# Sub-keys of the last token group in another tile, dense tiles 736 bytes lower, and an order edge between key steps and a decoding

## The chip, the cores and the metric

The kernel runs on one core of one Trainium2 chip. The metric is the device time of one execution in microseconds (us), as the median of several runs.

## The reference, cut to what matters

One decoder layer for 1024 tokens of width 1024. A first half (modulated RMSNorm, one input projection, mLSTM heads and differential attention heads, output projection, gated residual) comes ahead. The second half is a product-key retrieval of experts, and the change lies there:

```python
def block(xb):                                  # 128 tokens
    q = (xb @ w_query).reshape(128, 8, 2, 128)
    s = jnp.einsum('thpk,hpnk->thpn', q, sub_keys)
    sv, si = lax.top_k(s, 16)
    cand = (sv[:, :, 0, :, None] + sv[:, :, 1, None, :]).reshape(128, 8, 256)
    cidx = (si[:, :, 0, :, None] * 128 + si[:, :, 1, None, :]).reshape(128, 8, 256)
    fv, fpos = lax.top_k(cand, 16)
    eidx = jnp.take_along_axis(cidx, fpos, axis=-1)
    g = jax.nn.softmax(fv, axis=-1)
    act = gelu(jnp.einsum('td,thkd->thk', xb, u_tab[eidx]))
    return jnp.einsum('thk,thkd->td', g * act, v_tab[eidx])
```

Each token so picks 16 of 16384 experts in each of 8 heads, and adds their rows of `v_tab` with weights. A residual and a final RMSNorm follow.

## The kernel before, in words

The 1024 tokens are 8 blocks of 128, in three groups: blocks 0 and 1, blocks 2 to 4, blocks 5 to 7. Each group goes through its front: projections and heads (`front_proj`, `front_mix`, `front_out`), `keys_load` (line 816, loads the sub-keys into two tiles `sk`), `front_norm2` (line 821: second norm, the transposed rows `h2T`, and for dense blocks a copy of them in HBM, `hT_d`) and `front_keys` (line 842). That last one makes four steps g of four half-heads each. A step projects the queries (`proj_T`, matmuls `ps_pj` of line 391, with the query weights `wr` loaded by SP in line 373, 32 loads in all for a group), evacuates them with ACT into `qp`, multiplies them with the sub-keys (`ps_s`, line 862), evacuates the scores (`s`, line 870), and takes the top 16 on DVE (`key_tops`, line 877, and `top16`). After a block's last step `found` (line 1442) decodes the picks (`route`, line 919).

The expert rows are then worked in two ways.

- Blocks 0, 1, 6 and 7 gather their rows. POOL issues indirect DMAs: `gu` (line 1006) for the rows of u, whose products DVE sums row by row (line 1010); `gv` (line 1058) for the rows of v of blocks 0 and 1, summed on PE (line 1072); `gvr` (line 1039) for those of blocks 6 and 7, summed on DVE (line 1046). Lines 1162 to 1180 close a gathered block (`gy`, `xo`: residual and final norm).
- Blocks 2 to 5 are dense. `gates` (line 1193) makes a 128 x 16384 matrix of gates for each out of one-hots: `gh` (line 1202), `oh` on DVE (lines 1237, 1238), `ps_g` on PE (line 1224), a copy on ACT (`stg`, line 1226) and a store to HBM (`G_d`, line 1229). Then `dense` (line 1253) sweeps over all 16384 experts in 128 steps j for the 512 tokens. It loads the transposed rows (`hTld`, line 1299) and splits them into a high part on ACT and a rest on DVE (`dhT`, lines 1300 and 1301). A step `s_mm` (line 1307) loads `u` (line 1310), splits it (`us`: ACT in line 1312; in line 1313 POOL in the first 18 steps, DVE after) and issues 24 matmuls `ps_dS` (line 1320) with a gelu behind them. A step `s_gate` (line 1323) multiplies with the gates `Gt`, loaded by `load_G` (line 1267), and a `v_step` (line 1340) loads and splits `dv`, and adds into `ps_dA` (line 1352). The sweep starts with 14 steps of `s_mm` (`AHEAD`), before the first `s_gate`; from the fourth of them on, three pieces of block 5's gates are traced behind each (`late`):

```python
        for j in range(AHEAD):
            with later(-HP if j < HJ else 0):
                s_mm(j)
            if j >= L0:
                for _ in range(LG):
                    with later(-LP), behind(LPACE):
                        next(late, None)
```

The order of instructions on each engine is not written out. The program is traced in the order of its text with a priority for each instruction (the sweep stands behind the front by `later(PD)`, and the late gates are put ahead by `later(-LP)`), and a scheduler picks, on each engine, the first by priority of those that its own model of times holds ready. So what an instruction must wait for decides where it stands. Besides data, a place in SBUF counts: tiles of the fronts and of the sweep are put at the same addresses, and the first write of a later tile must wait for the last reader of an earlier one that it overlaps. In the last group, blocks 5, 6 and 7 take each key step in this order. SP and POOL issue DMAs in the order of their lists.

In the program before, `dhT` takes bytes 110656 to 143424 of each partition, and the last group's two `sk` tiles lie at 114304 to 118400 and at 120448 to 124544. The tiles `g` end at 109920. The tile for transposed rows at 171872 to 184160 (tag `mT` or `hT`) is free in the last group's keys; `h2T` lies in the other one, at 184160 to 196448.

Of the kernel before, what the change touches and what calls it, by code (L numbers as in the profile page):

```python
# [8 lines left out]
F32 = mybir.dt.float32  # L9
# [12 lines left out]
P = 128  # L22
# [29 lines left out]
def kernel(ctx: ExitStack, tc: tile.TileContext, x, c_col, ada_w, ada_b, ada_bc, n1c,  # L52
# [223 lines left out]
    @contextmanager  # L276
    def behind(engines):

        traced = nc.cur_bb.bb.instructions
        n = len(traced)  # L280
        anchors = {}
        for i in reversed(traced[max(0, n - 600):]):
            if i.engine not in anchors and i.name not in own:
                anchors[i.engine] = i.name
                if len(anchors) == 5:
                    break
        yield
        info = mybir.DependencyInfo(mybir.DependencyClass.NoSync, mybir.DependencyReason.DATA)
        for i in traced[n:]:
            own.add(i.name)  # L290
            if i.engine in engines and i.engine in anchors:
                tc.add_manual_dep(i, anchors[i.engine], info, reason="pace")

    def tick():

# [354 lines left out]
    def group(t0, nb):  # L650
        o = Group()
        o.t0, o.nb, o.n = t0, nb, nb * P
        o.tr = [slice((t0 + b) * P, (t0 + b + 1) * P) for b in range(nb)]
        return o

# [158 lines left out]
            proj_R(w_out, half * 512, mT, nb, y_evac(half))  # L814

    def keys_load(o):
        o.sk = [fr.tile([P, 8, P], F32, tag="c8", name="sk", bufs=C8) for _ in range(2)]
        for i in range(2):
            nc.sync.dma_start(o.sk[i], skT[:, i * 8:i * 8 + 8, :])

# [21 lines left out]
    def front_keys(o, found):  # L842

        n, nb = o.n, o.nb
        o.rt = [route_start() for _ in range(nb)]
        for g in range(4):
            if g == N1G and o.k + 1 < len(gs):
                front_norm1(gs[o.k + 1])
            sk = o.sk[g // 2][:, g % 2 * 4:g % 2 * 4 + 4]
            q = {}  # L850

            def q_evac(f, ps):
                t = fr.tile([P, 512], F32, tag="t2", name="qp", bufs=T2)
                for i in range(f.stop - f.start):
                    q[f.start + i] = t[:, i * n:i * n + n]
                nc.scalar.activation(t[:, :(f.stop - f.start) * n].rearrange("p (f n) -> p f n", n=n), ps, AF.Copy)

            proj_T(wq, g * 512, o.h2T, nb, q_evac)
            for b in o.order:
                ps = bank("ps_s")  # L860
                for f in range(4):
                    nc.tensor.matmul(ps[:, f * P:(f + 1) * P], q[f][:, b * P:(b + 1) * P], sk[:, f],
                                     start=True, stop=True)
                if b == o.put_off:
                    if g == 0:
                        kept = fr.tile([P, 16, P], F32, tag="stg", name="s", bufs=SB)
                    s = kept[:, g * 4:g * 4 + 4]
                else:
                    s = fr.tile([P, 4, P], F32, tag="t2", name="s", bufs=T2)
                nc.scalar.activation(s, ps.rearrange("p (f n) -> p f n", f=4), AF.Copy)  # L870
                if b != o.put_off:
                    key_tops(o, b, g, s, found)
        if o.put_off is not None:
            for g in range(4):
                key_tops(o, o.put_off, g, kept[:, g * 4:g * 4 + 4], found)
# [377 lines left out]
    def dense(d1, d2, d3, d4, psS, psA):  # L1253
# [4 lines left out]
        NH = -(-n // 512)  # L1258
        hw = n // NH
        Gt = {}  # L1260
        d1.tile([P, 256], F32, name="pad")

        def load_G(j, parts=((0, na // TS),)):
            if parts[0][0] == 0:
# [169 lines left out]
    for k, o in enumerate(gs):  # L1434
        front_proj(o)
        front_mix(o)
        front_out(o)
        keys_load(o)
        front_norm2(o)
        last = k + 1 == len(gs)  # L1440

        def found(b, h0=0, nh=PH):
            tb, r = o.t0 + b, o.rt[b]
            dense_ = tb in DENSE
            route(r, dense_, tb in MIXED or (dense_ and last), h0, nh)
            if not dense_:
                if h0 == 0:
                    waiting.append(g_start(tb, r))
                    o.rt[b].blk = waiting[-1]
                indices(r.blk, h0, nh)  # L1450
                if not streams:
                    streams.append(gathers())
                    background.append([streams[0], RG, 0.0])
            elif h0 + nh == PH:
                gating.append((r.ii, r.g.rearrange("p h k -> p (h k)"), DENSE.index(tb), False))

        o.order = sorted(range(o.nb), key=lambda b: ((o.t0 + b in DENSE) != (last and ORDL), b))
        o.soon = o.order if SOG[k] else []
        o.part = SOG[k]
        o.put_off = o.order[-1] if k == 0 and DEF else None  # L1460
        front_keys(o, found)
        if not last:
            front_T(gs[k + 1])
        for b in o.order:
            if b not in o.soon:
                found(b)
        if k == 0:
            tables = all_gates()
            background.append([tables, RP, 0.0])
# [72 lines left out]
```

## Time and profile before

| | |
|---|---|
| median of 3 runs | 3030.85 us (3019.99 to 3034.86) |
| profiled execution | 3014.83 us, span 3012.7 us |
| PE busy | 2795.3 us (93% of the span) |
| DVE busy | 2382.6 us (79%) |
| POOL busy | 1280.1 us (42%) |
| ACT busy | 971.3 us (32%) |
| DMA | 900.00 MB, mean 299 GB/s |

Times within the profile are microseconds from the start of the span. The keys of the last group run up to about 1420, the dense sweep from there to the end. [...] A row of the timeline gives the start, the length and the engine of a run of like instructions. SPq is the queue of SyncE, which issues most DMAs; PEld are the weight loads of PE.

### The profile page before, as it was taken

How to read it: one execution, taken by the hardware profiler on the slowest of the kernel's cores; microseconds unless marked ns; L12 is line 12 of the kernel's file. 1: busy time of each engine (PE TensorE's matmuls, PEld its weight loads, DVE VectorE, ACT ScalarE, POOL GpSimd, SP SyncE). 2: the span in 40 equal slices, each digit the busy share in tenths (PEclk: the TensorE clock that was granted, in tenths of full speed). 3: DMA queues.
4: the chain of work that ended last, by engine and by line, in shares of the span. 5: the costliest groups of instructions: out<-in, count | busy, mean ns of one | idle time of the engine just before them, and what ended most of it. 6: DMA issues, size and time to landing. Idle time of an engine off the chain costs nothing.

```text
span 3012.7 us, 40060 instructions
## 1 busy us (share of the span) xinstructions
PE 2795.3 (93%) x13686; PEld 2087.7 (69%) x13686; DVE 2382.6 (79%) x5489; ACT 971.3 (32%) x1692; POOL 1280.1 (42%) x1083
## 2 busy tenths in 40 slices
PE   6899999599999989999797999999999999999998
PEld 5547757375566756665475877788777787777886
DVE  5634999847997677356998988899888899888956
ACT  1432244311244444222443322323222223222332
POOL 0000366654565443334556555455444454444300
PEclk9989999699999979999798999999999999999999
DMA  8745699899999887988799999999999999999942
GB/s 281 248 141 178 227 359 331 312 365 337 321 347 323 298 296 275 342 318 312 281 312 321 332 323 320 336 343 322 330 321 335 326 344 321 322 317 311 307 140 70
DMA packets 396848, 900.00 MB, mean 299 GB/s; under 512 B 34770, under 2 KB 184274, under 8 KB 392548
## 3 DMA queue, kind: packets, MB, share of 16 engines
q0 software_dynamic: 147456, 536.94, 49.6%
q1 hardware_dynamic: 249188, 360.51, 35.8%
q8 instruction: 108, 1.77, 0.2%
q14 instruction: 96, 0.79, 0.1%
HBM read 846.97 MB, written 50.35 MB: 298 GB/s over the span
## 4 chain that ended last, share of the span: by engine, by line
PE 44%; DVE 27%; DMA 15%; issue 9%; ACT 2%; POOL 2%; SPq 0%; DVEq 0%; POOLq 0%; ACTq 0%
PE ps_pj L391 10%; PE ps_pj L411 8%; PE ps_dA L1352 7%; DVE gu L1010 7%; DMA Gt<-G_d 6%; PE ps_dS L1320 6%; DVE ga L1046 4%; PE ps_g L1224 3%; PE ga L1072 3%; DMA gu<-in_peer_u_dram,ei 2%; DVE dvs L1346 2%; PE ps_S L593 2%; DVE dacc L1359 2%; DVE us L1313 2%; DVE W L1331 1%
## 5 line engine op out<-in xcount | busy, mean ns | idle before, releaser
L1006 POOL DMA_INDIRECT gu<-in_peer_u_dram,ei x512 | 651.7, 1273 | 958.7 <-DVE sv L894 346.6
L1352 PE MATMUL ps_dA<-dvs,W 128*128 128x512 f32 x2976 | 718.5, 396 | 46.2 <-DVE dvs L1346 18.5
L1320 PE MATMUL ps_dS<-dhT,us 128*128 128x512 f32 x3072 | 733.4, 393 | 11.1 <-POOL us L1313 8.9
L1010 DVE SCALAR_TENSOR_TENSOR gu<-gu,h2r 128x1024 f32<-128x1024 f32 x512 | 630.0, 1241 | 74.6 <-DMA gu<-in_peer_u_dram,ei 66.0
L1352 PEld LDWEIGHTS ps_dA<-dvs,W 128*128 128x128 f32 x2976 | 566.2, 191 | 176.5 <-DVE dvs L1346 22.3
L1320 PEld LDWEIGHTS ps_dS<-dhT,us 128*128 128x128 f32 x3072 | 581.7, 190 | 138.2 <-POOL us L1313 10.3
L1039 POOL DMA_INDIRECT gvr<-in_peer_v_dram,ei x256 | 302.4, 1181 | 314.2 <-DVE ga L1046 178.3
L1058 POOL DMA_INDIRECT gv<-in_peer_v_dram,eT x256 | 274.6, 1073 | 263.1 <-PE ga L1072 143.1
L1046 DVE SCALAR_TENSOR_TENSOR ga<-gvr,w,ga 128x1024 f32<-128x1024 f32 x254 | 325.3, 1281 | 1.5 <-DVE us L1313 0.4
L1345 ACT ACTIVATE dvs<-dv 128x512 fp32r<-128x512 f32 x248 | 155.2, 626 | 323.3 <-PE ps_dA L1352 169.7
L391 PE MATMUL ps_pj<-hT,wr 128*128 128x384 f32 (+1 forms) x768 | 234.7, 461 | 2.8 <-ACT ae L586 2.6
L391 PE MATMUL ps_pj<-h2T,wr 128*128 128x384 f32 (+1 forms) x768 | 231.2, 454 | 0.0
L1321 ACT ACTIVATE ge<-ps_dS 128x512 f32<-128x512 f32 x128 | 76.5, 598 | 441.7 <-PE ps_dS L1320 430.2
L1226 ACT ACTIVATE stg<-ps_g 128x512 f32<-128x512 f32 x128 | 133.9, 1065 | 242.4 <-PE ps_g L1224 162.9
L391 PEld LDWEIGHTS ps_pj<-hT,wr 128*128 128x128 f32 x768 | 145.4, 194 | 79.9 <-issue 9.0
L1329 DVE SCALAR_TENSOR_TENSOR ge<-ge,Gt 128x512 f32<-128x512 f32 x128 | 86.5, 685 | 137.2 <-DMA Gt<-G_d 115.2
L391 PEld LDWEIGHTS ps_pj<-h2T,wr 128*128 128x128 f32 x768 | 142.2, 190 | 74.4 <-issue 11.1
L411 PE MATMUL ps_pj<-wr,hT 128*128 128x256 f32 (+1 forms) x672 | 179.9, 421 | 4.6 <-DMA wr<-in_w_in_dram 3.7
L1346 DVE TENSOR_TENSOR dvs<-dv,dvs 128x512 fp32r<-128x512 f32 x248 | 168.1, 682 | 16.9 <-ACT dvs L1345 16.9
L1237 DVE TENSOR_TENSOR oh<-iotah,dT 128x1024 f16<-128x1024 f16 x128 | 92.0, 724 | 111.7 <-PE ps_g L1224 90.4
L1224 PE MATMUL ps_g<-oh 128*128 128x128 f16 x1024 | 138.6, 296 | 33.3 <-DVE oh L1238 14.5
L1072 PE MATMUL ga<-gv,strip 128*32 128x256 f32 x2048 | 150.7, 410 | 15.4 <-DMA gv<-in_peer_v_dram,eT 11.7
(292 smaller groups left out, 3304.0 us busy)
## 6 DMA issues: line engine op xcount, KB each, us to landing
u<-in_peer_uT_dram SPq DMA_DIRECT2D x128, 512.0 KB
dv<-in_peer_v_dram SPq DMA_DIRECT2D x248, 256.0 KB
wr<-in_w_in_dram SPq DMA_DIRECT2D x168, 256.0 KB
G_d<-stg SPq DMA_DIRECT2D x32, 1024.0 KB
Gt<-G_d SPq DMA_DIRECT2D x15, 2048.0 KB
wmod<-in_ada_w_dram SPq DMA_DIRECT2D x48, 512.0 KB
wr<-in_peer_w_query_dram SPq DMA_DIRECT2D x96, 256.0 KB
wr<-in_w_out_dram SPq DMA_DIRECT2D x48, 256.0 KB
```

The lines of the kernel that those rows point to most:

```text
L391: nc.tensor.matmul(out[f], w2[:, kh, f * P:(f + 1) * P], hT[:, kb, :n], start=kb == 0 and f % k == 0, stop=kb == NC - 1 and f % k == k - 1)
L411: nc.tensor.matmul(out[f], hT[:, kb, f * P:(f + 1) * P], wk[:, kh], start=kb == 0 and f % k == 0, stop=kb == NC - 1 and (f % k == k - 1 or ...
L1006: nc.gpsimd.indirect_dma_start(out=u, out_offset=None, in_=pu, in_offset=bass.IndirectOffsetOnAxis(ap=o.ei[:, k:k + 1], axis=0))
L1010: nc.vector.scalar_tensor_tensor(u, u, 1.0, o.h2, op0=OP.mult, op1=OP.mult, accum_out=o.z[:, k:k + 1])
L1039: nc.gpsimd.indirect_dma_start(out=vt, out_offset=None, in_=pv, in_offset=bass.IndirectOffsetOnAxis(ap=o.ei[:, k:k + 1], axis=0))
L1046: nc.vector.scalar_tensor_tensor(o.acc, vt, o.w[:, k:k + 1], o.acc, op0=OP.mult, op1=OP.add)
L1058: got = nc.gpsimd.indirect_dma_start(out=vt, out_offset=None, in_=pv, in_offset=bass.IndirectOffsetOnAxis(ap=o.eT[:, t:t + 1], axis=0))
L1072: mm = nc.tensor.matmul(o.acc[c * 32:(c + 1) * 32, q * QW:(q + 1) * QW], st[:, q, 31 + 32 * i - r:63 + 32 * i - r], vt[:, c * QW:(c + 1) * ...
L1224: nc.tensor.matmul(pg[:, r * P:(r + 1) * P], oh[:, 0, :, r], oh[:, 2 + i, :, r], start=i == 0, stop=i == np_ - 1)
L1320: nc.tensor.matmul(ps, us[:, a, c], hT[:, b, c, sl], start=c == 0 and i == 0, stop=c == NC - 1 and i == 2)
L1346: nc.vector.tensor_sub(vs[:, 1], v, vs[:, 0])
L1352: nc.tensor.matmul(pacc[tb], w[:, a, tb * P:(tb + 1) * P], vs[:, b], start=jj == 0 and i == 0, stop=jj == J - 1 and i == 2)
```

## The change

It has three parts. The last group's sub-keys go into one tile `skl` with the tag of the transposed rows, instead of two tiles with the tag `c8`; it lies at 171872 to 180064. The unused tile `pad` at the start of the sweep's first pool shrinks from 256 to 72 floats, so that all the sweep's tiles lie 736 bytes lower: `dhT` now takes 109920 to 142688, and begins where the tiles `g` end. And a new helper `after` puts an order edge, without a semaphore, on every DVE instruction of a `key_tops` that is traced after block 5's decoding: each of them may stand only behind the last DVE instruction of that decoding. Since block 5 is the first in each key step, these are the last key steps (g = 3) of blocks 6 and 7.

```diff
+    @contextmanager
+    def after(anchor):
+
+        traced = nc.cur_bb.bb.instructions
+        n = len(traced)
+        yield
+        if anchor is not None:
+            info = mybir.DependencyInfo(mybir.DependencyClass.NoSync, mybir.DependencyReason.DATA)
+            for i in traced[n:]:
+                if i.engine == ET.DVE:
+                    tc.add_manual_dep(i, anchor, info, reason="the dense block's routing goes first")
...
     def keys_load(o):
-        o.sk = [fr.tile([P, 8, P], F32, tag="c8", name="sk", bufs=C8) for _ in range(2)]
+        if o.k + 1 < len(gs):
+            o.sk = [fr.tile([P, 8, P], F32, tag="c8", name="sk", bufs=C8) for _ in range(2)]
+        else:
+            sk = fr.tile([P, 16, P], F32, tag="mT", name="skl", bufs=2)
+            o.sk = [sk[:, 0:8], sk[:, 8:16]]
         for i in range(2):
             nc.sync.dma_start(o.sk[i], skT[:, i * 8:i * 8 + 8, :])
...
                 if b != o.put_off:
-                    key_tops(o, b, g, s, found)
+                    with after(o.anchor):
+                        key_tops(o, b, g, s, found)
...
         Gt = {}
-        d1.tile([P, 256], F32, name="pad")
+        d1.tile([P, 72], F32, name="pad")
...
         def found(b, h0=0, nh=PH):
+            decode(b, h0, nh)
+            if last and o.t0 + b in DENSE and h0 + nh == PH:
+                o.anchor = next(i.name for i in reversed(nc.cur_bb.bb.instructions) if i.engine == ET.DVE)
+
+        def decode(b, h0, nh):
             tb, r = o.t0 + b, o.rt[b]
```

The lines of the changed program stand 12 to 18 lower; line 1299 is 1317, line 1010 is 1028, and so on. The scheduler's order moves with the change at three places.

On SP, at the end of the last group's query weights (`wr`), before: the sweep's loads `hTld` and `u` stand behind the last of them.

```order
L373 DMA wr<-in_peer_w_query_dram 128x2x256 x4
L1229 DMA G_d<-stg 128x2048 x2
L1299 DMA hTld<-hT_d 128x1024 x2
L1229 DMA G_d<-stg 128x2048
L1299 DMA hTld<-hT_d 128x1024 x2
L1310 DMA u<-in_peer_uT_dram 128x1024
```

The same list in the changed program, from 11 of the 32 query-weight loads on:

```order
L385 DMA wr<-in_peer_w_query_dram 128x2x256
L1317 DMA hTld<-hT_d 128x1024 x2
L385 DMA wr<-in_peer_w_query_dram 128x2x256 x2
L1247 DMA G_d<-stg 128x2048
L385 DMA wr<-in_peer_w_query_dram 128x2x256
L1317 DMA hTld<-hT_d 128x1024 x2
L385 DMA wr<-in_peer_w_query_dram 128x2x256 x5
L1328 DMA u<-in_peer_uT_dram 128x1024 x2
```

The `hTld` loads have moved ahead of 20 and 17 of the query-weight loads, and the first two `u` ahead of 12.

On POOL, where the first splits `us` of the sweep enter the gathers `gv` of block 1, before:

```order
L1058 DMA gv<-in_peer_v_dram,eT 128x1024 x118
L1313 TENSOR_TENSOR us<-u,us 128x1024 x2
L1058 DMA gv<-in_peer_v_dram,eT 128x1024 x4
L1313 TENSOR_TENSOR us<-u,us 128x1024
L1058 DMA gv<-in_peer_v_dram,eT 128x1024 x4
```

And in the changed program:

```order
L1076 DMA gv<-in_peer_v_dram,eT 128x1024 x54
L1331 TENSOR_TENSOR us<-u,us 128x1024
L1076 DMA gv<-in_peer_v_dram,eT 128x1024 x2
L1331 TENSOR_TENSOR us<-u,us 128x1024
L1076 DMA gv<-in_peer_v_dram,eT 128x1024 x36
L1331 TENSOR_TENSOR us<-u,us 128x1024
L1076 DMA gv<-in_peer_v_dram,eT 128x1024 x5
```

The first two splits have moved ahead of 64 and 62 gathers that they stood behind; the third stands behind 36 more.

On DVE, among the one-hots `oh` of block 5's gates, before (`gu,z` is a row sum of block 6):

```order
L1237 TENSOR_TENSOR oh<-iotah,dT 128x1024
L1238 TENSOR_TENSOR oh<-oh,dT 128x1024
L1010 SCALAR_TENSOR_TENSOR gu,z<-gu,h2r 128x1024
L1238 TENSOR_TENSOR oh<-oh,dT 128x1024
L1010 SCALAR_TENSOR_TENSOR gu,z<-gu,h2r 128x1024
L1237 TENSOR_TENSOR oh<-iotah,dT 128x1024 x2
L1238 TENSOR_TENSOR oh<-oh,dT 128x1024
```

And in the changed program, near the end of the one-hots:

```order
L1255 TENSOR_TENSOR oh<-iotah,dT 128x1024
L1256 TENSOR_TENSOR oh<-oh,dT 128x1024
L1028 SCALAR_TENSOR_TENSOR gu,z<-gu,h2r 128x1024 x2
L1255 TENSOR_TENSOR oh<-iotah,dT 128x1024 x3
L1256 TENSOR_TENSOR oh<-oh,dT 128x1024 x3
L1028 SCALAR_TENSOR_TENSOR gu,z<-gu,h2r 128x1024 x2
```

Between `gh` and the last one-hot stood 19 row sums of block 6; 4 stand there now, and the others follow behind. On PE, behind the last `ps_s` of the keys, one set of `ps_g` and sums of `gv` are now followed at once by 24 and 6 `ps_dS`, and then by 7 or 8 of them between sets of 8 `ps_g`; of the 384 `ps_dS` ahead of the first `ps_dA`, 39 stood behind the last `ps_g`, and none does now.

## Rows read from the trace of the kernel before

**Rows 1.** Windows: busy us (instructions) by engine, PE's clock, DMA share, GB/s.

```profile
core 0: us, PE busy (x) PEld busy (x) DVE busy (x) ACT busy (x) POOL busy (x), PEclk, DMA share, GB/s
1268.00:1413.80 145.80, 145.80 (x966) 87.87 (x965) 89.32 (x459) 36.76 (x51) 58.00 (x58) 1.00 0.88 308
...
1420.00:1494.30 74.30, 47.49 (x352) 29.18 (x350) 67.45 (x249) 29.08 (x29) 43.26 (x33) 0.72 0.86 314
1494.30:1607.50 113.20, 104.04 (x619) 83.36 (x620) 107.03 (x189) 58.73 (x65) 66.41 (x42) 0.94 0.87 289
1607.50:1638.80 31.30, 13.27 (x55) 10.15 (x54) 22.66 (x33) 5.70 (x8) 23.64 (x16) 0.74 0.97 352
1700.00:2000.00 300.00, 293.52 (x1271) 241.01 (x1270) 268.53 (x411) 89.18 (x135) 160.20 (x123) 0.98 0.94 331
...
2830.00:2930.00 100.00, 100.00 (x443) 82.81 (x442) 58.76 (x78) 33.40 (x49) 0.94 (x1) 1.00 0.57 186
```

**Rows 2.** Timeline, end of block 5's gates and first `ps_dA`: start, us, engine, line.

```profile
1606.38 0.68 DVE L1238 TENSOR_TENSOR oh<-oh,dT 128x1024 f16<-128x1024 f16 x1
...
1608.92 1.10 PE L1224 MATMUL ps_g<-oh 128*128 128x128 f16 x8
...
1611.26 0.33 SPq L1229 DMA_DIRECT2D G_d<-stg  x1
...
1638.78 1.65 PE L1352 MATMUL ps_dA<-dvs,W 128*128 128x512 f32 x3 [12.55 <-ACT W L1330]
```

**Rows 3.** Sources L1046 (last gathered rows) and L1313 (POOL splits): ns min/median/max, starts.

```profile
L1046 DVE SCALAR_TENSOR_TENSOR ga<-gvr,w,ga x254: 1268/1280/1291, 1897.3 to 2841.4; 128x1024 f32<-128x1024 f32 x127
...
L1313 POOL TENSOR_TENSOR us<-u,us x18: 2347/2640/3378, 1466.9 to 1630.6; 128x1024 fp32r<-128x1024 f32 x18
```

**Rows 4.** Timeline, first dense loads, last scores of the keys, first splits.

```profile
1416.21 1.39 SPq L1299 DMA_DIRECT2D hTld<-hT_d  x2
...
1418.98 2.94 PE L862 MATMUL ps_s<-sk,qp 128*128 128x128 f32 x24
...
1435.16 2.00 ACT L1300 ACTIVATE dhT<-hTld 128x1024 fp32r<-128x1024 f32 x2
...
1455.65 0.33 SPq L1310 DMA_DIRECT2D u<-in_peer_uT_dram  x1
...
1458.95 0.37 SPq L1310 DMA_DIRECT2D u<-in_peer_uT_dram  x1
...
1464.21 1.04 ACT L1312 ACTIVATE us<-u 128x1024 fp32r<-128x1024 f32 x1
...
1468.53 1.06 ACT L1312 ACTIVATE us<-u 128x1024 fp32r<-128x1024 f32 x1 [3.29 <-DMA u<-in_peer_uT_dram]
```

**Rows 5.** Groups of DVE in the sweep, 1700 to 2800: busy us, mean ns, idle.

```profile
L1046 DVE SCALAR_TENSOR_TENSOR ga<-gvr,w,ga 128x1024 f32<-128x1024 f32 x235 | 300.9, 1281 | 1.3 <-DVE us L1313 0.4
...
L1010 DVE SCALAR_TENSOR_TENSOR gu<-gu,h2r 128x1024 f32<-128x1024 f32 x201 | 241.8, 1215 | 4.9 <-DMA gu<-in_peer_u_dram,ei 4.9
```

**Rows 6.** Groups of DVE from 1420 to 1607.5.

```profile
L1010 DVE SCALAR_TENSOR_TENSOR gu<-gu,h2r 128x1024 f32<-128x1024 f32 x19 | 31.8, 1682 | 0.0
L1238 DVE TENSOR_TENSOR oh<-oh,dT 128x1024 f16<-128x1024 f16 x37 | 31.1, 867 | 0.0
L1237 DVE TENSOR_TENSOR oh<-iotah,dT 128x1024 f16<-128x1024 f16 x37 | 29.7, 813 | 6.4 <-PE ps_g L1224 6.4
...
L1301 DVE TENSOR_TENSOR dhT<-hTld,dhT 128x1024 fp32r<-128x1024 f32 x4 | 4.9, 1217 | 0.8 <-ACT dhT L1300 0.8
```

**Rows 7.** Sources L1172 and L1180, closing of gathered blocks, on DVE.

```profile
L1172 DVE SCALAR_TENSOR_TENSOR gy<-xo x8: 411/418/458, 1185.8 to 1546.7; 128x256 f32<-128x256 f32 x8
...
L1180 DVE SCALAR_TENSOR_TENSOR xo<-xo,gms,g2f x8: 477/480/485, 1192.5 to 1555.9; 128x256 f32<-128x256 f32 x8
```

**Rows 8.** Timeline of DVE, a row sum during a POOL split.

```profile
1598.48 3.42 DVE L1010 SCALAR_TENSOR_TENSOR gu<-gu,h2r 128x1024 f32<-128x1024 f32 x1
```

**Rows 9.** Groups of PE from 1422 to 1638.

```profile
L1320 PE MATMUL ps_dS<-dhT,us 128*128 128x512 f32 x384 | 99.8, 415 | 11.1 <-POOL us L1313 8.9 <-ACT us L1312 2.2
```

More of the change, by code (lines that the diff above doesn't have):

```diff
@@ L652, in group @@
         o.t0, o.nb, o.n = t0, nb, nb * P
+        o.anchor = None
         o.tr = [slice((t0 + b) * P, (t0 + b + 1) * P) for b in range(nb)]
```

## The prediction, made before the changed kernel ran

> **What bounds the kernel now.** I read the windows first. [Rows 1] cut the stretch in which the last group's keys end and the dense sweep of blocks 2 to 5 starts. In the keys stage (1268 to 1413.8 us) PE is busy all the time: 145.8 of 145.8 us. In the sweep itself (1700 to 2000) it is busy 293.5 of 300. Between them lies a hole: 47.5 of 74.3 us, 104.0 of 113.2 and 13.3 of 31.3. PE thus stands idle 26.8 + 9.2 + 18.0 = 54 us, while DVE is busy 67.5 of 74.3 and 107.0 of 113.2 us, 174.5 of 187.5 together. So the hole is bounded by DVE up to the last one-hot, which starts at 1606.4, and then by a chain: last `ps_g`, stage copy, store of G_d at 1611.3, load of it, gate product, first `ps_dA` at 1638.8 [rows 2]. Behind that the sweep runs on PE to its end, with gathers beside it until 2841 [rows 3] and without them after (226 ns a matmul there, 100 us over 443, against 236, 300 over 1271, [rows 1]). Whatever brings the first `ps_dA` forward therefore comes off the end, apart from what follows below.
>
> **Why the dense sweep's first steps lie in the hole.** The timeline of the queues [rows 4] shows that the first two loads of `hTld` are issued at 1416.2 and split at 1435.2, only after the last score matmuls of the keys (1419.0, 2.9 us). The address that `dhT` gets covers the last group's two sub-key tiles, so its first write must wait for the last matmul that reads them. The first `u` is issued at 1455.7 and split at 1464.2, and the first `ps_dS` comes behind that.
>
> **The change, part by part.**
>
> *Sub-keys in the other tile, dense tiles 736 bytes lower.* Both together let `dhT` begin where the gate tiles `g` end and no longer meet the sub-keys. By themselves they cost no instruction: two loads of the same size into another tile. The order is what changes. On SP the `hTld` loads move from behind all 32 query-weight loads to behind 12 and 15 of them, the first `u` behind 20. On POOL two of the 18 splits (`us`) move ahead of the keys' end. On PE 24 `ps_dS` and 6 more follow the last score matmuls almost directly; the 16 steps (384 `ps_dS`) still all stand before the first `ps_dA`, but none any more behind the last `ps_g`, where 39 stood. And on DVE the row sums `gu` of block 6, which now gets its gathers later because POOL still issues block 1's, shrink from 19 to 4 between `gh` and the last one-hot.
>
> What leaves the 187.5 us on DVE:
> - 15 row sums at their undisturbed 1.215 us [rows 5]: 18.2 us.
> - 4 splits of `dhT`, 4.9 us [rows 6], which go into the keys stage, where DVE is busy 89.3 of 145.8 us [rows 1]: covered there.
> - The last two gathered blocks' closing operations, now behind the last one-hot: 4 at 0.42 and 4 at 0.48 us [rows 7], 3.6 us. There DVE is idle 31.3 - 22.7 = 8.6 us, so they are covered; without the cover they would cost the 3.6.
> - What two POOL splits do to DVE, now ahead of 1420. The trace does not show that cost as a row; it is bounded by 0 and by 2 x 2.6 us (a split's whole length, [rows 3]). A row sum beside a split took 3.42 us at 1598.5 instead of 1.215 [rows 5, 8], so I take the difference, 2.2 each: 4.4 us.
> - Added: one more pair of one-hots, 0.81 + 0.87 = 1.7 us [rows 6].
>
> Sum: 18.2 + 4.9 + 3.6 + 4.4 - 1.7 = 29.4 us, and 174.5 would become 145. With the 13 us of idle time that DVE had, the stretch would be 158.
>
> [...]
>
> PE sets a second floor. It was busy 47.5 + 104.0 = 151.5 us in that stretch, and the 39 `ps_dS` from behind come in at about 0.24 us, 9 us: 161. So the stretch can shrink by 187.5 - 161 = 26 us at the prices of before. The granted clock was 0.72 in its first part [rows 1], and 384 `ps_dS` took 415 ns each by the record, 99.8 us [rows 9]; at the 236 ns of the sweep they would be 90.6. With PE kept busy, 9 us more could come. I don't count on it: PE still has to wait for one-hots and splits in turn.
>
> So the floors of the two engines allow 26 (PE) and 29 (DVE). Two engines that feed one another never both run without idle time; PE waited 11.1 us for splits alone [rows 9]. I take 2 to 3 us for that, and 24 remain.
>
> *What is given back later.* Block 6's row sums and all gathers behind them come later, by as much as the 15 that left: 15 gathers, some 38 us at the pace of the sweep (201 + 235 row operations in 1100 us, 2.5 us each, [rows 5]), and with the sweep starting 24 us earlier the gathers stand beside 62 us more of it. Beside gathers a matmul costs 4.4% more (236 against 226 ns): 2.7 us. The gathers end near 2880, still over 100 us before the end, so they don't become the bound.
>
> *The order edge (key step 3 of blocks 6 and 7 behind block 5's decoding).* Between block 5's own last key step and `gh` DVE has 190 instructions before and 189 after; four of the difference are the `dhT` splits and the rest one-hots. Block 6's keys and their decoding stand before `gh` as they did. So I price the edge at nothing. It could only cost if it held the other blocks' keys and made the gathers later, and those have 100 us to spare.
>
> *The tail behind the last `ps_g`* keeps its instructions: store, load, product. From 1608.9 to 1638.8, 30 us, unchanged [rows 2].
>
> **Sum.** 24 - 2.7 = 21 to 22 us. The profiled execution took 3014.8 us, 16 below the median of the three runs, 3030.9. Against its own time that gives about 2993, and against the median, in which the next runs will be told, 3009.
>
> **Rivals.**
>
> *A, slower: loads that block the keys stage.* SP and ACT work in order. The `hTld` loads now stand in the middle of the query-weight loads, and on ACT their splits and the first two of `us` stand between the evacuations of the keys' projections and scores. In [rows 4] an `hTld` came to its split 19.0 us after its issue, a `u` after 8.6 and 9.6. If ACT waits so in the new place, PE runs out of free banks, and in this stage PE has no idle time to give: twice 19.0 and twice 9 are 56 us in the worst case. Against it: the loads are issued long before their splits are due by the order, and the 19 us contain the wait for the sub-keys, which is gone. It decides from 24 us of PE idle time in 1268 to 1420 upwards; with 40 us of it the time would be 3047.
>
> *B, no change: the same work, waits in another place.* In the new order PE has 7 or 8 `ps_dS` between each set of one-hot matmuls. [...] DVE waited 6.4 us for `ps_g` already [rows 6]. If the 13 us idle become 35, the gain is 22 less, and 3028 to 3031 comes out. In its favour stand the 16 splits left, 2.6 us each; against it, that `dhT` and the first two splits are ready by 1420, so that PE starts ahead.
>
> *C, a larger gain.* If PE runs the stretch at full clock, the 9 us come on top, and if DVE loses its idle time too, the stretch is 145 us: a gain of 35 to 40, less 3: 2994 to 2999. The 54 us of idle PE time are the end of this side: 2980.
>
> *D, the order edge does not act or the lower tiles do not matter.* The order shows the moves, so only the price can fail; this falls under B.
>
> **How the numbers follow.** About 0.5%, 15 us, is what a measurement of this kernel can tell from no change; three runs lay 15 us apart. Forecast (gain of 15 to 28): 0.46. C: 0.18. B, with D and partial losses (gain under 15): 0.25. A: 0.11. Faster is the forecast with C, 0.64; same is B, 0.25; slower is A, 0.11. The range leaves out most of A and the end of C: 2984 to 3028.
>
> **What would show it.** Right: `hTld` issued before 1300; the first `ps_dS` within 5 us of the last score matmuls; PE idle in the keys stage under 3 us; PE's clock above 0.9 in the 75 us behind it; the last one-hot 22 to 28 us earlier, near 1580, and the first `ps_dA` near 1613; last row of the gathers near 2880. Wrong: PE idle in the keys stage by ACT's or SP's waits (A); last one-hot still near 1605 with DVE waiting for `ps_g` (B); or an early first `ps_dA` and yet the same end, which would say that the sweep's pace, not its start, sets the time.

## The result, and the profile after

The changed kernel takes 2989.23 us (median of 4 runs, 2983.2 to 2997.83) against 3026.49 us before (4 runs of the same series): ratio 0.9867, 95% interval [0.9844, 0.9891]. That is 37 us less, where the forecast gain was 21 to 22 us; the forecast's own ratio, 3009 to 3030.85, is 0.993, outside that interval. The time lies in the range that was given; the size of the gain was underestimated. The profiled execution took 2983.2 us with a span of 2981.3, 31.4 us below the span of before.

The windows of the changed kernel, in the stretches of [rows 1]: busy us (instructions) of each engine, PE's granted clock as a share of its full speed, DMA share, GB/s.

```profile
1268.00:1413.80 145.80, 145.80 (x955) 88.68 (x954) 97.36 (x480) 42.20 (x59) 59.49 (x54) 1.00 0.88 310
...
1420.00:1494.30 74.30, 68.66 (x452) 44.77 (x445) 72.97 (x240) 39.53 (x40) 48.09 (x35) 0.95 0.79 275
1494.30:1607.50 113.20, 86.68 (x604) 66.27 (x602) 84.35 (x122) 47.16 (x53) 57.52 (x41) 0.89 0.87 311
1607.50:1638.80 31.30, 26.02 (x98) 20.73 (x99) 28.00 (x48) 10.44 (x16) 10.89 (x9) 0.80 0.76 246
1700.00:2000.00 300.00, 297.53 (x1302) 245.00 (x1301) 269.03 (x414) 89.72 (x135) 164.88 (x124) 0.99 0.96 338
```

In the first 74 us behind the keys PE is now busy 68.7 us instead of 47.5, at a granted clock of 0.95 instead of 0.72. The row from 1607.5 is a trap: what stood at 1607 to 1638 before stands 28 us earlier now. Where a change moves work, stretches between the same instructions compare better. The same view of the kernel before, cut at the last scores of the first key step (1302.3), at those of the last (1421.9), at the last one-hot (1606.4) and at the first `ps_dA` (1638.8):

```profile
1302.30:1421.90 119.60, 119.35 (x833) 72.01 (x831) 81.08 (x450) 30.43 (x40) 51.87 (x52) 1.00 0.87 299
1421.90:1606.40 184.50, 148.52 (x949) 109.86 (x948) 172.28 (x430) 85.94 (x91) 107.21 (x74) 0.85 0.87 300
1606.40:1638.80 32.40, 14.37 (x60) 11.06 (x58) 23.76 (x35) 5.89 (x8) 24.50 (x17) 0.75 0.96 347
```

And of the changed kernel, cut at the same four instructions:

```profile
1302.40:1411.30 108.90, 108.90 (x722) 66.05 (x722) 82.70 (x448) 30.89 (x43) 47.73 (x44) 1.00 0.86 298
1411.30:1578.50 167.20, 161.25 (x1094) 114.98 (x1093) 146.60 (x384) 81.81 (x85) 92.79 (x67) 0.98 0.83 295
1578.50:1610.70 32.20, 2.48 (x19) 2.02 (x17) 20.50 (x37) 7.20 (x11) 16.86 (x13) 0.57 0.87 316
```

From the first scores to the first `ps_dA` it was 336.5 us and is 308.3: 28.2 less. PE's busy time went from 282.2 to 272.6 (9.6 less), its idle time from 54.3 to 35.7 (18.6 less), DVE's busy time from 277.1 to 249.8. Of the 35.7, 29.7 lie in the last row, behind the last one-hot. The work between these instructions is nearly the same, but not quite: of the one-hot products 24 fewer stand there (3.2 us at 0.132 us each), and of the sums of `gv` 16 more (1.2 us at 0.078). Before, then in the changed kernel:

```profile
L1224 PE MATMUL ps_g<-oh 128*128 128x128 f16 x464 | 61.2, 296 | 18.2 <-DVE oh L1238 8.9 <-ACT stg L1226 5.5 <-DVE cand L913 3.7
L1072 PE MATMUL ga<-gv,strip 128*32 128x256 f32 x720 | 55.9, 427 | 8.6 <-DMA gv<-in_peer_v_dram,eT 8.0 <-issue 0.6
...
L1242 PE MATMUL ps_g<-oh 128*128 128x128 f16 x440 | 58.5, 296 | 0.3 <-issue 0.3
L1090 PE MATMUL ga<-gv,strip 128*32 128x256 f32 x736 | 54.4, 394 | 0.3 <-DMA gv<-in_peer_v_dram,eT 0.3
```

The timeline of the changed kernel shows the mechanism, against [rows 4]: the loads of `hTld` are issued 131 us earlier, `dhT` is split while the keys still run, and the first `ps_dS` follow the last scores with 1.9 us between them, where it was 43 us.

```profile
1285.38 1.46 SPq L1317 DMA_DIRECT2D hTld<-hT_d  x2
...
1296.17 1.05 ACT L1318 ACTIVATE dhT<-hTld 128x1024 fp32r<-128x1024 f32 x1
...
1410.80 0.49 PE L879 MATMUL ps_s<-skl,qp 128*128 128x128 f32 x2
...
1413.15 3.01 PE L1338 MATMUL ps_dS<-dhT,us 128*128 128x512 f32 x12
```

Sources of the changed kernel, in the manner of [rows 3]: POOL splits, last gathered rows.

```profile
L1331 POOL TENSOR_TENSOR us<-u,us x18: 2355/2396/2932, 1332.3 to 1584.2; 128x1024 fp32r<-128x1024 f32 x18
...
L1064 DVE SCALAR_TENSOR_TENSOR ga<-gvr,w,ga x254: 1276/1287/1297, 1906.7 to 2857.2; 128x1024 f32<-128x1024 f32 x127
```

Groups of DVE in the changed kernel, from the last scores to the last one-hot (1411.3 to 1578.5), against [rows 6]:

```profile
L1255 DVE TENSOR_TENSOR oh<-iotah,dT 128x1024 f16<-128x1024 f16 x38 | 38.0, 1011 | 18.4 <-PE ps_g L1242 18.4
L1256 DVE TENSOR_TENSOR oh<-oh,dT 128x1024 f16<-128x1024 f16 x38 | 25.1, 685 | 0.2
...
L1028 DVE SCALAR_TENSOR_TENSOR gu<-gu,h2r 128x1024 f32<-128x1024 f32 x4 | 4.7, 1221 | 0.0
```

The row sums went from 19 to 4, as the order said. DVE now waits 18.4 us for `ps_g` instead of 6.4. And on PE, from the first scores to the first `ps_dA`, against [rows 9]:

```profile
L1338 PE MATMUL ps_dS<-dhT,us 128*128 128x512 f32 x384 | 97.6, 402 | 1.2 <-POOL us L1331 1.2
...
L1370 PE MATMUL ps_dA<-dvs,W 128*128 128x512 f32 x1 | 0.8, 792 | 27.4 <-ACT W L1348 27.4
```

The waits for splits (11.1 us before) are gone to 1.2, and one long wait is left, 27.4 us ahead of the first `ps_dA`. The timeline shows what it is, against [rows 2]: the last store of gates, the load of them 9.5 us behind it, and the gate product 17.6 us behind the load.

```profile
1582.18 0.33 SPq L1247 DMA_DIRECT2D G_d<-stg  x1
...
1591.69 0.76 SPq L1285 DMA_DIRECT2D Gt<-G_d  x1
...
1609.29 4.30 DVE L1347 SCALAR_TENSOR_TENSOR ge<-ge,Gt 128x512 f32<-128x512 f32 x7 [6.89 <-DMA Gt<-G_d]
...
1610.70 2.07 PE L1370 MATMUL ps_dA<-dvs,W 128*128 128x512 f32 x4 [27.35 <-ACT W L1348]
```

### The profile page after: what moved, and what is told of

Its sections match the earlier page's. It is cut to its first block, busy times and chain, and to the rows that moved or that the text cites. A ratio compares the mean times of both kernels' runs of the same rounds, so it can differ in the third digit from the quotient of the medians.

```text
span 2981.3 us, 40087 instructions
## 1 busy us (share of the span) xinstructions
PE 2783.4 (93%) x13686; PEld 2076.9 (70%) x13686; DVE 2382.0 (80%) x5489; ACT 973.6 (33%) x1695; POOL 1282.8 (43%) x1083
## 4 chain that ended last, share of the span: by engine, by line
PE 50%; DVE 18%; DMA 13%; issue 11%; POOL 5%; ACT 2%; SPq 0%; DVEq 0%; POOLq 0%; ACTq 0%
PE ps_pj L403 11%; PE ps_dS L1338 9%; PE ps_dA L1370 9%; DMA Gt<-G_d 8%; PE ps_pj L423 7%; DVE gu L1028 4%; PE ps_g L1242 3%; PE ga L1090 3%; POOL gvr L1057 3%; DVE ga L1064 2%; DMA gu<-in_peer_u_dram,ei 2%; PE ps_S L605 2%; DVE dvs L1364 1%; DMA gv<-in_peer_v_dram,eT 1%; PE ps_tr L379 1%
## 5 line engine op out<-in xcount | busy, mean ns | idle before, releaser
L1370 PE MATMUL ps_dA<-dvs,W 128*128 128x512 f32 x2976 | 720.8, 396 | 56.9 <-ACT W L1348 27.4
L1370 PEld LDWEIGHTS ps_dA<-dvs,W 128*128 128x128 f32 x2976 | 566.1, 191 | 188.9 <-ACT W L1348 27.4
L1028 DVE SCALAR_TENSOR_TENSOR gu<-gu,h2r 128x1024 f32<-128x1024 f32 x512 | 620.1, 1222 | 72.3 <-DMA gu<-in_peer_u_dram,ei 59.1
L1255 DVE TENSOR_TENSOR oh<-iotah,dT 128x1024 f16<-128x1024 f16 x128 | 102.2, 804 | 118.5 <-PE ps_g L1242 94.7
L1364 DVE TENSOR_TENSOR dvs<-dv,dvs 128x512 fp32r<-128x512 f32 x248 | 171.9, 698 | 16.4 <-ACT dvs L1363 16.4
L423 PEld LDWEIGHTS ps_pj<-wr,hT 128*128 128x128 f32 x672 | 128.5, 197 | 45.4 <-issue 23.8
L1377 DVE TENSOR_TENSOR dacc<-dacc,ps_dA 128x512 f32<-128x512 f32 x240 | 156.1, 683 | 4.6 <-PE ps_dA L1370 4.6
```

The lines of the kernel that those rows point to most:

```text
L423: nc.tensor.matmul(out[f], hT[:, kb, f * P:(f + 1) * P], wk[:, kh], start=kb == 0 and f % k == 0, stop=kb == NC - 1 and (f % k == k - 1 or ...
L1028: nc.vector.scalar_tensor_tensor(u, u, 1.0, o.h2, op0=OP.mult, op1=OP.mult, accum_out=o.z[:, k:k + 1])
L1364: nc.vector.tensor_sub(vs[:, 1], v, vs[:, 0])
L1370: nc.tensor.matmul(pacc[tb], w[:, a, tb * P:(tb + 1) * P], vs[:, b], start=jj == 0 and i == 0, stop=jj == J - 1 and i == 2)
L1377: nc.vector.tensor_add(o, o, pacc[tb])
```

## The experiments

Theory 1 was: the gain comes from the end of the overlap between `dhT` and the sub-keys; PE gets dense steps to do while DVE makes block 5's one-hots, and what is left of the hole is PE's order and the chain behind the last one-hot. The rivals stand with each run. All profiles are cut at the same instructions as above; the columns are us between them.

| run | to first scores | keys, first to last scores | to last one-hot | to first `ps_dA` | sweep to the end | span |
|---|---|---|---|---|---|---|
| before | 1302.3 | 119.6 | 184.5 | 32.4 | 1373.9 | 3012.7 |
| e1 pad alone | 1306.1 | 119.9 | 184.1 | 32.8 | 1376.9 | 3019.8 |
| e4 edge and pad | 1311.7 | 120.7 | 175.9 | 30.1 | 1376.7 | 3015.1 |
| changed | 1302.4 | 108.9 | 167.2 | 32.2 | 1370.6 | 2981.3 |
| e2 without the pad | 1302.8 | 108.9 | 165.6 | 30.6 | 1366.7 | 2974.6 |
| e3 without the edge | 1307.6 | 108.9 | 163.9 | 29.0 | 1374.7 | 2984.1 |
| e5 `ps_dS` held | 1300.9 | 109.9 | 149.0 | 33.0 | 1366.6 | 2959.4 |
| e6 load split | 1307.7 | 108.9 | 165.4 | 27.1 | 1377.4 | 2986.5 |
| e7 both | 1311.8 | 108.9 | 149.8 | 34.8 | 1366.0 | 2971.3 |
| e8 splits on DVE | 1311.7 | 112.7 | 166.5 | 27.9 | 1377.6 | 2996.4 |
| e9 held, no edge | 1304.3 | 110.3 | 147.5 | 26.9 | 1368.3 | 2957.3 |
| e10 held less, split, no edge | 1315.0 | 108.9 | 150.9 | 29.4 | 1379.3 | 2983.5 |
| e11 fewer gathers | 1306.8 | 108.9 | 165.4 | 31.9 | 1355.1 | 2968.1 |

The first column varies by 14 us between programs whose order there is the same up to that point or nearly so, and the sweep by 11 us within nearly one order (e2 and e6): that is the scatter of single executions. The part from the first scores to the first `ps_dA` scatters less: 336.5 and 336.8 us in the two profiles of the old order (before, e1), 308.3 and 305.1 in two of the new (changed, e2). So it became 28 to 32 us shorter.

### e1: the pad alone

```diff
-        d1.tile([P, 256], F32, name="pad")
+        d1.tile([P, 72], F32, name="pad")
```

> The kernel before with only the sweep's tiles 736 bytes lower; the sub-keys stay in their two old tiles, and no order edge. Theory 1 (the end of the address overlap between dhT and the sub-keys makes the gain): dhT still meets the old sub-key tiles, so the order is that of before and nothing moves: last one-hot near 1606, first ps_dA near 1639, time within 0.5% of before (3011 to 3042). Rival (addresses themselves, or the row tile a2r that dhT no longer meets, matter): first hTld before 1416 and 10 us or more gained. Beside that it is a second profile of the order of before: how far its sweep, from first ps_dA to the end, lies from 1373.9 us, tells how much of the 3.3 us by which the changed kernel's sweep was shorter is scatter.

Measured: 3026.97 us, ratio 1.0014 [0.9996, 1.0031] against 3023.05 us (19 runs). No part of the kernel moves by more than the scatter. The lower tiles alone do nothing.

### e2: sub-keys and edge, the pad as before

```diff
-        d1.tile([P, 72], F32, name="pad")
+        d1.tile([P, 256], F32, name="pad")
```

> The changed kernel with the pad back at 256 floats: sub-keys in the other tile and the order edge. The order on every engine is that of the changed kernel. Theory 1: dhT now ends 448 bytes inside the row tile a2r, which is last read before the keys begin, so it costs nothing: last one-hot near 1578, first ps_dA near 1611, ratio to before near 0.987. Rival: the 736 bytes carry part of the gain, then 5 us or more are lost against the changed kernel and hTld or dhT show a wait in 1280 to 1320. Second profile of the changed order: its sweep from first ps_dA to the end against 1370.6.

Measured: 2980.14 us, ratio 0.9868 [0.9845, 0.9891], the same as the changed kernel's. So the 736 bytes carry nothing: the overlap that mattered is that with the sub-keys, and the one with the row tile does not.

### e3: the change without the order edge

```diff
-                    with after(o.anchor):
+                    with after(None):
```

> The changed kernel without the order edge. Theory 1: the edge is worth nothing, since between gh and the last one-hot DVE has 127 instructions with 4 row sums here, 126 with 4 in the changed kernel: last one-hot 1576 to 1581, ratio to before 0.984 to 0.990. Rival (the edge brings block 5's gates forward): gh 5 us or more later than 1483, last one-hot as much later.

Measured: 2985.59 us, ratio 0.9887 [0.9859, 0.9915]. The intervals lie over one another, so with the sub-keys moved the edge is not to be told from nothing. In the table the part from the last scores to the last one-hot is even 2 to 3 us shorter without it; the one-hots' last was expected between 1576 and 1581 and came at 1580.4. Since e1 shows the pad to be worth nothing, this run is close to the move of the sub-keys alone. It also bears on what paces the one-hots: DVE is busy 139.6 us there, 7.0 less than in the changed kernel (146.6), and the part is only 3.3 us shorter.

### e4: edge and pad, sub-keys in their old tiles

```diff
-        if o.k + 1 < len(gs):
+        if True:
             o.sk = [fr.tile([P, 8, P], F32, tag="c8", name="sk", bufs=C8) for _ in range(2)]
```

> The kernel before with the order edge and the lower tiles, sub-keys in their two old tiles: dhT still waits for the last score matmuls. Theory 1: no gain from it, hTld issued after 1400, 17 row sums ahead of the last one-hot, first ps_dA 1628 to 1640, time within 0.5% of before. Rival (DVE is relieved by the edge): last one-hot 10 us or more earlier than 1606.

Measured: 3011.97 us (10 runs), ratio 0.9956 [0.9939, 0.9974]: 11 us faster, which neither theory had. Its windows, from the first scores on:

```profile
1311.70:1432.40 120.70, 119.58 (x833) 71.99 (x831) 81.01 (x451) 30.15 (x40) 51.94 (x52) 1.00 0.85 296
1432.40:1608.30 175.90, 142.98 (x919) 103.90 (x919) 164.60 (x423) 81.20 (x86) 97.18 (x70) 0.85 0.89 305
1608.30:1638.40 30.10, 22.18 (x90) 17.12 (x88) 23.75 (x31) 9.62 (x14) 23.00 (x15) 0.87 0.92 319
```

`dhT` is as late as before (the keys take 120.7 us, PE's clock behind them is 0.85), yet the one-hots end 8.6 us sooner behind the last scores (175.9 against 184.5), and PE is busy 22.2 us instead of 14.4 in the last part, since 72 `ps_dS` stand behind the last `ps_g` there and 39 did before. Since e1 shows the pad to be worth nothing, this is the edge: it shifts the whole order of the late gates. So my price of nothing holds only beside the moved sub-keys. DVE's busy time in that part falls by 7.7 us, and its row sums alone from 31.8 us (19 at 1682 ns) to 22.8 (17 at 1347). Why they are cheaper in the new order was not followed further.

### e5: dense steps from 11 on held behind the last gates

```diff
         for j in range(AHEAD):
-            with later(-HP if j < HJ else 0):
+            if j == 11:
+                with later(-LP):
+                    for _ in late:
+                        pass
+                hold = next(i.name for i in reversed(nc.cur_bb.bb.instructions) if i.engine == ET.PE)
+            with later(-HP if j < HJ else 0), held(hold):
                 s_mm(j)
```

`held` puts an order edge like that of `after` on the PE instructions traced within it; steps 14 and 15 get it too.

> The changed kernel, with the ps_dS of the steps from 11 on ordered behind block 5's last ps_g on PE; 264 ps_dS stand ahead of it and 120 behind. Theory 1 (what is left of the hole is PE's: DVE waited 18.4 us for ps_g, and PE then stands idle 27.4 us ahead of the first ps_dA): last one-hot 10 to 18 us after 160 instead of 167 us from the keys' end, that is near 1563 where the keys end at 1411, PE busy in the 32 us behind it, first ps_dA near 1595, ratio to before 0.979 to 0.984. Rival (DVE sets the one-hots' pace, the waits are only gaps of it): last one-hot stays 167 us behind the keys' end, 120 ps_dS fill the tail for nothing, ratio 0.986 to 0.990.

Measured: 2965.22 us, ratio 0.9807 [0.9779, 0.9834]. From the last scores to the last one-hot it is 149.0 instead of 167.2 us, and the first `ps_dA` comes 16.4 us earlier behind the first scores (291.9 against 308.3). The windows, cut at the last scores (1410.8), the last one-hot and the first `ps_dA`:

```profile
1410.80:1559.80 149.00, 133.77 (x977) 93.44 (x975) 140.95 (x380) 75.89 (x77) 86.62 (x64) 0.94 0.87 311
1559.80:1592.80 33.00, 31.57 (x137) 25.07 (x136) 28.07 (x44) 15.89 (x21) 23.06 (x16) 0.92 0.96 336
```

DVE, busy 146.6 of 167.2 us in the changed kernel, is busy 141.0 of 149.0 here, and waits 6.3 us for `ps_g`:

```profile
DVE oh L1267 <- PE ps_g L1254: 6.3, 5, 2.9
```

Of the 18.2 us, 12.6 are idle time of DVE (20.6 against 8.0) and 5.6 its busy time: 11 POOL splits stand in that part instead of 14, and the first half of a one-hot takes 820 instead of 1011 ns. So in the changed kernel the one-hots were paced for the most part by PE, which did dense steps between them; the same steps fit in the 33 us in which PE waits for the gates' store and load. Theory 1 holds, and the bound passes back to DVE.

### e6: the last load of gates in three parts

```diff
-            load_G(0, ((early, na // TS),))
+            load_G(0, ((early, early + 4), (early + 4, na // TS - 1), (na // TS - 1, na // TS)))
```

> The changed kernel, with the last load of block 5's gates (eight token parts, 17.6 us from its issue to the first product) cut into three loads of 4, 3 and 1 parts, so that only the last eighth waits for the last store. Theory 1 (the tail behind the last one-hot is a chain of store, landing, load): the tail of 32.2 us becomes 20 to 25 us and as much comes off the end, ratio 0.983 to 0.985. Rival (the load's time is queueing behind gathers, not its size): tail 29 to 33 us, ratio as the changed kernel, 0.987.

Measured: 2985.9 us, ratio 0.9864 [0.9835, 0.9894]: no gain to be seen. The tail went from 32.2 to 27.1 us in the profile, 5 us instead of the 7 to 12 expected; and since it is 29.0 to 32.2 us in the four profiles without the split (changed, e2, e3, e11), as little as 2 of them may be the split's. The timeline of DVE ahead of the first product:

```profile
1602.29 1.23 DVE L1028 SCALAR_TENSOR_TENSOR gu<-gu,h2r 128x1024 f32<-128x1024 f32 x1 [3.33 <-DMA gu<-in_peer_u_dram,ei]
...
1606.53 1.23 DVE L1028 SCALAR_TENSOR_TENSOR gu<-gu,h2r 128x1024 f32<-128x1024 f32 x1
...
1607.68 4.92 DVE L1347 SCALAR_TENSOR_TENSOR ge<-ge,Gt 128x512 f32<-128x512 f32 x8
```

The product no longer waits for the load: it follows a row sum without a gap. Four row sums stand ahead of it on DVE, and wait for gathers themselves. Part of what the load gave went into this queue.

### e7: both

The edits of e5 and e6 together.

> Both of the last two in one kernel. If each works by itself and they add up: last one-hot near 1563, tail 20 to 25 us, first ps_dA near 1585, ratio 0.975 to 0.980. If the 120 ps_dS behind the last ps_g (28 us at 0.235) are longer than the shorter tail, PE sets it and the gain of the split load is lost: ratio as e5.

Measured: 2970.98 us, ratio 0.9811 [0.9786, 0.9835], as e5. The tail is 34.8 us, with PE busy 32.6 of it: the 120 `ps_dS` are longer than the chain that they cover, so the split load has nothing to give.

### e8: the first 18 splits on DVE

`UP`, the number of splits that POOL takes, goes from 18 to 0. DVE takes them: at the 1223 ns that its 110 other splits `us` take in the mean in the changed kernel, 18 are 22 us.

```diff
-    WB, T2, C8, KV, T4, RB, SB, OB, WLO, PB, LAG, DB, GD, AHEAD, LG, RH, ORDL, UP, LP, L0, DU, HP, HJ = 7, 8, 4, 2, 3, 3, 1, 2, 0, 5, 4, 2, 1, 14, 3, 4, 1, 18, 310000, 3, 28, 0, 0
+    WB, T2, C8, KV, T4, RB, SB, OB, WLO, PB, LAG, DB, GD, AHEAD, LG, RH, ORDL, UP, LP, L0, DU, HP, HJ = 7, 8, 4, 2, 3, 3, 1, 2, 0, 5, 4, 2, 1, 14, 3, 4, 1, 0, 310000, 3, 28, 0, 0
```

> [...] If a POOL split holds DVE for 2.2 us (my term of the sum), 16 of them in the stretch cost 35 us now, and taking them away and paying 22 leaves the last one-hot where it is or up to 13 us earlier. If they cost DVE little, the last one-hot comes up to 22 us later, less the 20 us in which DVE idled: later by 5 to 22 us, ratio 0.989 to 0.994. [...]

Measured: 2998.34 us, ratio 0.9904 [0.9872, 0.9936]. The part to the last one-hot is 166.5 us, as in the changed kernel (167.2), though DVE does 16 splits and 4 row sums more there. The window of that part and its groups on DVE:

```profile
1424.40:1590.90 166.50, 158.58 (x1094) 113.68 (x1092) 142.28 (x421) 86.00 (x89) 66.35 (x59) 0.98 0.89 314
...
L1255 DVE TENSOR_TENSOR oh<-iotah,dT 128x1024 f16<-128x1024 f16 x38 | 25.8, 690 | 17.4 <-PE ps_g L1242 15.9 <-issue 1.4
L1256 DVE TENSOR_TENSOR oh<-oh,dT 128x1024 f16<-128x1024 f16 x38 | 25.2, 688 | 0.0
L1331 DVE TENSOR_TENSOR us<-u,us 128x1024 fp32r<-128x1024 f32 x16 | 19.5, 1221 | 3.5 <-ACT us L1330 3.4
```

The first half of a one-hot takes 690 ns where it took 1011 beside POOL's splits: 38 x 0.32 = 12 us. Steps of the decoding and the small copies `strip` give another 17; the clearest of them, in the changed kernel and here:

```profile
L972 DVE TENSOR_TENSOR ii<-pr 128x128 f32<-128x128 f16 x6 | 6.6, 1106 | 0.1
...
L972 DVE TENSOR_TENSOR ii<-pr 128x128 f32<-128x128 f16 x6 | 1.7, 284 | 0.1
```

That is 29 us for the 14 splits that POOL did there, 2.1 each; I had taken 2.2. So POOL's splits do lengthen DVE's instructions here, by about what I had taken; by what mechanism, no run shows. Taking them off POOL is worth nothing in this part, because the splits themselves cost DVE 19.5 us and PE sets the pace, busy 158.6 of 166.5 us while DVE waits 17.4 us ahead of one-hots. The higher median would lie elsewhere, though the intervals still overlap: in the profile the keys take 3.8 us longer, and the sweep is at the long end.

### e9 and e10: held steps without the edge

e9 is e5 with `after(None)`. e10 holds from step 12 on, has the split load of e6, and no edge either.

> The kernel of e5 (ps_dS from step 11 on behind the last ps_g) without the order edge. Without the edge gh came 67.6 instead of 72.1 us behind the keys' end (e3 against the changed kernel). If the hole is DVE's in e5 (DVE busy 141 of 149 us there), the first ps_dA comes 3 to 5 us earlier behind the first scores than the 291.9 us of e5: 287 to 289, ratio 0.978 to 0.980. If the edge is worth nothing also here: 290 to 293, ratio as e5, 0.981.

> One step more of ps_dS ahead of the last ps_g (288 ahead, 96 behind, 23 us at 0.235), the last gate load in three parts, and no edge. If PE's 120 ps_dS set the tail of e7 (34.8 us, PE busy 32.6), 96 of them make it 28 to 30 us, and the last one-hot comes 0 to 6 us later than in e9: first ps_dA 283 to 291 us behind the first scores, ratio 0.976 to 0.981. Rival (the parts of the load wait for one another on the queue): tail 32 to 35 us.

Measured: e9 2962.3 us, ratio 0.9805 [0.977, 0.9839]; e10 2974.09 us, ratio 0.9829 [0.9797, 0.9861]. In e9 the first `ps_dA` comes 284.7 us behind the first scores, 7 us earlier than in e5, but most of that is order: 24 `ps_dS`, 5.6 us at 0.235, stand behind the first `ps_dA` in e9 that stand ahead of it in e5. In the time nothing shows beyond the intervals. e9 has the lowest median of all, 62 us below the kernel before; e5, e7 and e9 cannot be told apart. e10's tail of 29.4 us agrees with its 96 `ps_dS`, its one-hots with e5's, and it is no better.

### e11: 127 gathers fewer beside the sweep

```diff
+        out_ = o.tb == 7 and k > 0
+        if not out_:
             vt = gat.tile([P, D], F32, tag="gx", name="gvr", bufs=GB)
...
-            else:
+            elif not out_:
                 nc.vector.scalar_tensor_tensor(o.acc, vt, o.w[:, k:k + 1], o.acc, op0=OP.mult, op1=OP.add)
```

> The changed kernel without 127 of the 128 gathers of v rows of block 7 and without the DVE sums of these rows, so the output of that block lacks 127 of its 128 terms. It prices a gather beside the sweep. My term took 4.4% of a matmul's time (236 against 226 ns): 127 gathers at 2.5 us are 320 us of the sweep that go without, so the sweep is 12 to 16 us shorter than the 1367 to 1377 us of the changed order. Rival (matmuls wait for something else there, and the gathers fill gaps): less than 5 us.

Measured: 2971.53 us, ratio 0.9822 [0.9785, 0.986]. Its sweep is 1355.1 us; the four profiles of the changed order (changed, e2, e3, e6) have 1366.7 to 1377.4, 1372.4 in the mean. That is 17 us less, 12 to 22 by the scatter. The ratios say the same less sharply, 0.9822 against 0.9864 to 0.9887 with intervals that overlap. So a gather beside the sweep, with its sum on DVE, does cost what the prediction took for it, or somewhat more. The rows tell in which form. First the stretch without gathers here, then the one with them in the changed kernel, and what PE waited for within that (2540 to 2840):

```profile
2533.00:2846.00 313.00, 313.00 (x1382) 259.26 (x1382) 153.02 (x212) 100.37 (x149) 0.00 (x0) 1.00 0.42 130
...
2530.00:2857.00 327.00, 318.95 (x1374) 260.15 (x1373) 290.97 (x330) 96.17 (x144) 145.44 (x124) 0.98 0.93 325
...
L1370 PE MATMUL ps_dA<-dvs,W 128*128 128x512 f32 x624 | 153.1, 400 | 8.0 <-DVE dvs L1364 6.8 <-DVE dacc L1377 1.0
```

A matmul takes 226 ns without and 238 with them. Over 1374 matmuls that is 16 us: 8 of PE idle, mostly waiting for DVE's splits `dvs`, and 8 of busy time, at a clock of 0.98 instead of 1.00. The run takes gathers and sums away together, so how much belongs to the sums, which stand in DVE's queue beside `dvs`, is not shown.

## Why the prediction was right and wrong

**Right: the bound and the mechanism.** The hole between keys and sweep was the place, the overlap of `dhT` with the sub-keys its cause (e1 to e4), and 28 of the 31 us between the two profiles lie there. The signs held but for one, the last row of the gathers (below): `hTld` issued at 1285, first `ps_dS` 1.9 us behind the last scores, PE idle 0 us in 1268 to 1413.8 (rival A), clock 0.95 behind, last one-hot 28 us earlier at 1578.5, first `ps_dA` at 1610.7. Rival B's wait is there, 18.4 us of DVE for `ps_g` instead of 6.4, but it took only part of the gain.

**Right in size: DVE's sum.** 29.4 us were to leave DVE up to the last one-hot; from the last scores to the last one-hot it is 25.7 less (172.3 and 146.6). The parts are others. The row sums gave 27.1 us (31.8 and 4.7), not 18.2, because the 15 that left were not undisturbed ones but stood at 1682 ns in the mean. The `dhT` splits (4.9) and the closing operations (3.4) left and stayed covered, as I had it. The one-hots took 2.3 us back instead of 1.7, and `ii` and `jj` of the decoding 6.9 (2.5 and 9.4), which I did not foresee. POOL splits there are 14 against 15, one fewer and not two: what two would do, 4.4 us, was the right rate (e8) for one too many, and the splits that stay lengthen other instructions than before (the first halves of one-hots went from 813 to 1011 ns in the mean, the row sums from 1682 to 1221). In the sum the runs agree with the cost that I took for a split (2.1 us by e8 against 2.2); row by row they do not show it.

**Wrong: the step from the floors to 24.** I set PE's floor at 161 us "at the prices of before", said of the 9 us that a full clock would give "I don't count on it", and took 2 to 3 us for the two engines' waits. Measured between the same instructions it is 28.2 us (28 to 32 with e1 and e2), and the term that failed is the price. From the first scores to the last one-hot PE was busy 267.9 of 304.1 us before and 270.2 of 276.1 in the changed kernel. At the prices of before the work that now stands there would have taken 277 us: 50 `ps_dS` more at 0.24, 28 `ps_g` fewer at 0.132, 16 `ga` more at 0.078. So 7 us that I did not count came from the price, while the waits left were 6.0 us and not 2 to 3. The granted clock up to the last one-hot went from 0.85 to 0.98 with it, and PE's waits for splits from 11.1 to 1.2 us. The row in which I had looked for the 9 us, though, gave only 2.2 of them: the 384 `ps_dS` were busy 97.6 us instead of 99.8; the `ga` gave 2.7 (54.4 where 736 at 0.078 are 57.1), and the rest does not show in any one group. In size the gain is rival C's, to which I gave 0.18, but not by its way: DVE did not lose its idle time, which grew from 12.2 to 20.6 us ahead of the last one-hot.

There is a flaw in the frame, too: I kept the keys' end at 1420. It moved 10.7 us forward, since 80 matmuls of `ga` and 30 of `ps_g` fewer are done in the keys (336 against 416, and 122 against 152); the POOL order that I had read, splits ahead of 64 gathers, said so of the `ga`. These went behind the keys' end, where 400 stand against 304, and of the `ps_g` most now stand ahead of the first scores. Moving work so is no gain of its own; but it hides the true one from a sum that starts at a fixed time.

**Wrong: the 2.7 us given back.** The gathers end at 2857 instead of 2841, 1246.5 us behind the first `ps_dA` instead of 1202.6: 44 us more beside the sweep, not 62. At 4.4% that is 1.9 us, and e11 says that the rate is about right. But the sweep was not longer: 1370.6 and 1366.7 us in the new order (changed, e2) against 1373.9 and 1376.9 in the old (before, e1). The difference of 7 us in the means is of the size of the scatter of single profiles, so neither a cost nor a gain is shown there. What remains between the profiles' 31 us and the medians' 37 is within the scatter of runs: the profiled execution of before, 3014.83 us, lies below every one of the 19 runs beside e1 to e4 (3015.62 at the lowest), and the median of three to which I pinned the forecast, 3030.85, above their median of 3023.05. By these two profiles and the medians, the 16 us by which the gain exceeds the forecast are 4 from the step to 24, 6 from the sweep (2.7 not given back and 3.3 shorter) and 6 from the scatter of runs.

**The edge** was priced at nothing. With the sub-keys moved that is what e3 shows; without them it is worth 11 us (e4), which I did not foresee. Counting instructions up to `gh` did not tell that: 6.1 of e4's 8.6 us stand behind it (105.9 us from `gh` to the last one-hot, 112.0 before).

**The tail** was to stay at 30 us and did (32.4 and 32.2). That it would stand with PE idle for 27 us of it, because all 384 `ps_dS` now came ahead, was in the order that I quoted, and I did not price it. It is the largest piece that the change left lying, and e5 and e9 take it up.

## What to carry to other kernels

Sum a change between two instructions that it does not move, by the bound engine's busy and idle time, and not from a fixed time on. When an engine that idled gets work queued, look at the price of its instructions beside its waits; here PE's price fell by 7 us as its granted clock went from 0.85 to 0.98. And look where the new order leaves the next idle stretch: work that is free to wait should be kept for a wait that cannot be shortened, here 120 matmuls behind the last gates.

## What the runs showed of the hardware that was not expected

What POOL's splits cost DVE fell on other instructions in each of these orders. Row sums took 1682 ns in the mean before, against 1215 undisturbed, and the second halves of one-hots 867; in the changed kernel the first halves took 1011 and the second 685, and without the edge (e3) the first halves 717 and the four row sums 1768. With the splits off POOL (e8) the first halves take 690. One row's mean therefore says little of the next order's; the cost for each split, 2.1 us by e8, says more.

And 127 gathers with their sums take 17 us out of a sweep in which PE is busy 98% of the time (294.9 of 300 us from 1710 to 2010), 0.13 us for each gather, though PE is no part of a gather: about half of it as waits for DVE, half as busy time at a granted clock of 0.98 instead of 1.00.
